# A hybrid decoder step on one core: twelve prepended rows left out of all products after the inputs of convolution and pooling

## The chip, the cores and the metric

The kernel runs on one core of one Trainium2 chip. The metric is the device time of one execution, in microseconds (us). Three runs of the kernel before took 3000.92, 3002.06 and 3005.93 us; their median, 3002.06 us, is the time that the change is measured against.

The engines of the core have the names of the profile: PE multiplies matrices (PEld is its loading of weights, which overlaps), DVE and ACT do the elementwise work, POOL copies a few columns, and SP issues all DMAs, one after the other in its program's order.

## The reference, cut to what matters

One layer over 2064 prompt rows (16 learned rows are prepended to 2048 given ones) and over 64 sample rows (8 sequences of 8 rows, with their past given). D is 1024, F is 2816.

```
xp = concat([meta, x_prompt])                  # 16 + 2048 rows
h = rmsnorm(x, norm1_g);  z = h @ w_in         # 1024 -> 5 * 1024
za, zg, zp, gate_a, gate_b = split(z)
a = causal_dwconv(za * sigmoid(zg), conv_dw)   # 31 taps: row t reads rows t-30 .. t
a = silu(layernorm(a + conv_b)) @ w_conv_out
p = trailing means of zp over 2/4/8/16 rows, minus zp
p = (p @ w_pool, in 4 groups) * pool_scale
x = x + (sigmoid(gate_a) * a + sigmoid(gate_b) * p) @ w_out
up = causal_dwconv(rmsnorm(x, norm2_g) @ w_up, ffn_dw)   # 3 taps: rows t-2 .. t
x = x + (gelu(up[F:]) * up[:F]) @ w_down
y = rmsnorm(x, final_g);  y_prompt = y[16:]    # the 16 prepended rows are dropped
```

Beside y_prompt and y_sample the last rows of the inputs of both convolutions and of the pooling are returned. What a prepended row yields after the convolution and the pooling reaches an output in one way alone: the 3-tap convolution of row 16 reads the up-projected rows 14 and 15. The rows 0 to 13 act through za, zg and zp only.

## The kernel before, in words

Rows of x are the columns of all tiles: a tile is 128 channels by the rows of one block. The 2128 rows (2064 prompt, 64 sample) are cut into three blocks of 708, 708 and 712 (`WIDTHS`); the sample rows end the last one. A product of a block is done in two halves, `hw(b)` columns each, so its matmuls are 354 or 356 columns wide; the up-projection takes two columns more, of the block or half before, for its three taps (`halo=2`): 356 or 358.

Each product is made exact enough by three matmuls of fp32r operands: weights and rows are split into a high and a low part, and `gemm` multiplies low by high, high by low and high by high, for each of the K chunks of 128 and each half:

```
for i, (c0, c1) in enumerate(rng):
    o = ps[:, i, : c1 - c0]
    ...
    mm(o, wl[:, w0 : w0 + P], rh, k == 0, False)
    mm(o, wh[:, w0 : w0 + P], rl, False, False)
    mm(o, wh[:, w0 : w0 + P], rh, False, k == last)
```

`rng(b, ts_, halo)` gives the columns of each half. A unit is one output chunk of 128 channels: for K = 1024 it is 8 x 2 x 3 = 48 matmuls. The units stand in this order: gates and values of block 0, with those of block 1 between (`G_first`); pooling inputs, pooling maps and the two merge gates of block 0 (`PG`), its convolution's output product (`C`), `WO`, and the feed-forward part (`FF`: 44 up units and the down units in four groups); then `PG`, `C`, `WO` of block 1, `G` of block 2, `FF` of block 1; then `PG`, `C`, `WO`, `FF` of block 2. In block 2 all but three of the up-projection's pairs of chunks are done by a Strassen-like scheme of seven half-sized products (`pair`), whose mixed weights are made beforehand on ACT and DVE from `in_w_up` by the task `mixed_weights`: two loads into `raw` tiles, then six parts of it, each with two or more stores `keep<-s`, piece by piece wherever there is room.

Weights are split once, and the halves are stored (`keep<-wb`) and read back later (`wb<-keep`); four buffers `wb` are in use, and SP loads the next as soon as one is free. `final` ends a block: a norm, eight DVE multiplications and eight stores `out_y<-s`.

While it is built, the kernel keeps a model of the engines' time (`Pace`): whenever it holds DVE to be behind PE's planned work, `drip` emits pieces of side tasks (the 31 taps of `conv_norm`, norms, `mixed_weights`). So the place of each such piece in the queues of DVE, ACT and SP hangs on the planned widths. The order within a queue is fixed when the program runs.

In value and pool units `value_post` and `pool_post` write the result behind the history of 30 or 15 columns (zeros for block 0), and pooling's first 16 columns of block 0 are divided by the true count (`icnt`).

Of the kernel before, what the change touches and what calls it, by code (L numbers as in the profile page):

```python
# [26 lines left out]
N_META = 16  # L27
# [4 lines left out]

NBLK = 3
SBLK = 2
TOT = NP_ALL + NSAMP
_W = TOT // NBLK // 4 * 4
WIDTHS = [_W + 4 * (i >= NBLK - (TOT - NBLK * _W) // 4) for i in range(NBLK)]
assert sum(WIDTHS) == TOT and all(w % 4 == 0 for w in WIDTHS)
# [94 lines left out]
def trunk(ctx: ExitStack, tc: tile.TileContext, A, O):  # L133
# [45 lines left out]
    def tt(out, a, b, op):  # L179
        nc.vector.tensor_tensor(out=out, in0=a, in1=b, op=op)  # L180
        pace.put("dve", dve(out, 68 + 60 * (b.space == "PSUM")), [out], [a, b])

    def stt(out, a, s, b, op0, op1):
        nc.vector.scalar_tensor_tensor(out=out, in0=a, scalar=s, in1=b, op0=op0, op1=op1)  # L184
        pace.put("dve", dve(out, 68 if isinstance(s, float) else 129), [out], [a, b])
# [8 lines left out]
    def act(out, a, func, **kw):  # L194
        nc.scalar.activation(out, a, func, **kw)  # L195
        ptr = sum(not isinstance(v, float) for v in kw.values())
        pace.put("act", size(out) / 1.2 + 93 + 93 * ptr + 51 * (a.space == "PSUM"), [out], [a])

    def pcopy(out, a):
        nc.gpsimd.tensor_copy(out, a)  # L200
        pace.put("pool", 220.0, [out], [a])

    def load(out, src):
        nc.sync.dma_start(out=out, in_=src)  # L204
        pace.put("dma", size(out) * P * 4 / 340.0, [out], [], late=2000.0)
# [20 lines left out]
    def hcol(o):  # L226
        return half[:, o - O_LG : o - O_LG + 1]

    def hw(b):
        return WIDTHS[b] // 2  # L230

    def cols(b, ts_):
        return ts_[0] * hw(b), (ts_[-1] + 1) * hw(b)

    def sb(ap, b, ts_):

        c0, c1 = cols(b, ts_)
        return ap[:, c0:c1].rearrange("p (a c) -> p a c", a=len(ts_))

    def ps_of(ps, b, ts_, off=0):  # L240
        return ps[:, : len(ts_), off : off + hw(b)]

    R = {}

# [97 lines left out]
                mm(o, wh[:, w0 : w0 + P], rh, False, k == last)  # L342
            yield

    def rng(b, ts_, halo=0):
        h = hw(b)
        return [(t * h, (t + 1) * h + halo) for t in ts_]


    def at(ap):  # L350
# [74 lines left out]
    def x_load(b, c, c0=0, c1=None):  # L425
        c1 = WIDTHS[b] if c1 is None else c1
        x = S(c1 - c0)
        load(x, A["x"][c, :, COL0[b] + c0 : COL0[b] + c1])
        return x

    def staggered(first):
# [15 lines left out]

    def norm1_first(ts_):

        c0, c1 = cols(0, ts_)  # L450
        xs = [x_load(0, c, c0, c1) for c in range(KC)]
        yield at(xs[0])

        def src(c):
            yield
            return xs[c]

        r = yield from rstd_of(src, c1 - c0)
        if ts_[0] == 0:
            R["h", 0] = [(S(WIDTHS[0], F32R), S(WIDTHS[0], F32R)) for _ in range(KC)]  # L460
# [59 lines left out]

    def gate_post(b, c, ts_, ps):
        if ts_[0] == 0:
            R["t", b, c] = S(WIDTHS[b])
        act(sb(R["t", b, c], b, ts_), ps_of(ps, b, ts_), AF.Tanh, scale=0.5)
        yield

    def value_post(b, c, ts_, ps):
        n, h, t = NPB[b], hw(b), R["t", b, c]
        if ts_[0] == 0:
            a = S(HC + n)  # L530
            pcopy(a[:, :HC], ahist[:, c, :])
            R["a", b, c] = [a, None, 0]
        a = R["a", b, c][0]
        if n == WIDTHS[b]:
            stt(sb(a[:, HC:], b, ts_), sb(t, b, ts_), 1.0, ps_of(ps, b, ts_), ALU.add, ALU.mult)
        else:
# [12 lines left out]
        yield  # L549
# [120 lines left out]
    def pool_post(b, c, ps):  # L670
        W, h, n = WIDTHS[b], hw(b), NPB[b]
        samp = n != W
        g = c // 2
        u = S(HP + n)
        pcopy(u[:, :HP], phist[:, c, :])
        if samp:
            us = R.pop(("su", c))
            act(u[:, HP : HP + h], ps[:, 0, :h], AF.Copy)
            act(u[:, HP + h : HP + n], ps[:, 1, : n - h], AF.Copy)
            act(us[:, :, HP:], ps[:, 1, n - h : h].rearrange("p (a c) -> p a c", a=NS), AF.Copy)  # L680
            store(O["pool_s"][c], us)
        else:
            act(sb(u[:, HP:], b, BOTH), ps_of(ps, b, BOTH), AF.Copy)
        pcopy(phist[:, c, :], u[:, n : n + HP])
        yield at(u)

        def window(u):
# [12 lines left out]
        pf = S(W)  # L700
        inv = 1.0 / WINS[g]
        stt(pf[:, :n], cur[:, HP : HP + n], inv, u[:, HP : HP + n], ALU.mult, ALU.subtract)
        if samp:
            cs = window(us)
            o = pf[:, n:].rearrange("p (a c) -> p a c", a=NS)
            stt(o, cs[:, :, HP:], inv, us[:, :, HP:], ALU.mult, ALU.subtract)
        if b == 0:
            e = mpool.tile([P, 16], F32, tag="e", name=nm("e"), bufs=2)
            tt(e, cur[:, HP : HP + 16], cst[:, O_IC + 16 * g : O_IC + 16 * g + 16], ALU.mult)
            tt(pf[:, :16], e, u[:, HP : HP + 16], ALU.subtract)  # L710
# [408 lines left out]
    def W(key, src, n=None):  # L1119
        wq.append(Weight(key, src, n or src.shape[1]))  # L1120
        return len(wq) - 1
# [8 lines left out]
        t.start, t.after = start, after  # L1130
        order.append(t)

    def std_unit(w, pairs, b, ts_, post, needs=(), wait=False, halo=0, pre=None, drop=None, hold=None):
        box = []

        def mmf(w):
            if pre:
                pre()
            ps = hold.pop() if hold else PSUM()
            (box if hold is None or ts_ == SECOND else hold).append(ps)  # L1140
            yield from gemm(ps if hold is None else ps[:, ts_[0] :, :], w, pairs(), rng(b, ts_, halo))
            if drop:
                del R[drop]

        def after():
            ps = box.pop()
            yield at(ps)
            yield from post(ps)

        units.append(Unit(w, mmf, None if hold is not None and ts_ == FIRST else after, needs, wait))  # L1150

    def gate(b, c, w, nd, ts_=BOTH):
        std_unit(w, lambda: R["h", b], b, ts_, lambda ps: gate_post(b, c, ts_, ps), nd)

    def value(b, c, w, nd, ts_=BOTH, drop=False):
        std_unit(
            w, lambda: R["h", b], b, ts_, lambda ps: value_post(b, c, ts_, ps), nd,
            pre=past(b, "sa", c, HC, "st_conv", 3), drop=("h", b) if drop else None,
        )

    def w_gate(c):
# [437 lines left out]
```

## Time and profile before

| what | us |
|---|---|
| median of three runs | 3002.06 |
| the profiled execution, its own time | 3004.2 |
| its span, first to last instruction | 3002.1 |
| PE busy with matmuls (98% of the span) | 2938.3 |
| PEld busy with weights (97%) | 2924.6 |
| DVE busy (68%) | 2042.8 |
| ACT busy (27%) | 821.2 |
| POOL busy (4%) | 108.8 |

The profiled execution took 2.1 us more than its span and 2.1 us more than the median. The blocks' stages stand at these times: gates and values to 282 us, the rest of block 0 to 1154 us, block 1 (with the gates and values of block 2 within it) to 2150 us, block 2 to the end. Busy shares are means over all of it. A row of the timeline merges instructions of one kind that follow each other closely; "idle before" in brackets is the wait ahead of the first, and what ended it.

### The profile page before, as it was taken

Reading aid. Unit: us, or ns where it says so; the run is one execution under the profiler, and the core shown is the slowest. Engines: PE = TensorE matmul, PEld = TensorE weight load, DVE = VectorE, ACT = ScalarE, POOL = GpSimd, SP = SyncE. Lnnn points to the kernel's source line nnn. Section 1 sums busy time; section 2 is a strip of 40 time slices with the busy share of each in tenths; the row PEclk is TensorE's granted clock in tenths of the full one; section 3 lists DMA queues with packets and bytes.
Section 4 is the critical chain, followed back from the end, with each engine's and each line's share of the span. In section 5 each row is a group of like instructions: output and inputs, shape, how many; then the busy total and the mean of one; then the engine's idle time right before and its main releaser. Section 6 shows DMA issues by size and latency. Waiting matters only on the chain.

```text
span 3002.1 us, 44205 instructions
## 1 busy us (share of the span) xinstructions
PE 2938.3 (98%) x17928; PEld 2924.6 (97%) x17928; DVE 2042.8 (68%) x3006; ACT 821.2 (27%) x1238; POOL 108.8 (4%) x201
## 2 busy tenths in 40 slices
PE   7999999999999998999999999999999999999998
PEld 7999999999999998999999999999999999999997
DVE  7998998679996456653489999655652137544645
ACT  4201334233223232432221212223241113221312
POOL 0111100020000000000010000000000000000000
PEclk9999999999999999999999999999999999999999
DMA  7424554955655557888743444799743376777686
GB/s 283 160 71 161 196 207 162 335 212 173 229 189 197 204 191 286 274 321 277 277 154 120 163 136 146 266 320 328 266 170 138 139 267 215 255 268 263 236 302 242
DMA packets 187755, 660.41 MB, mean 220 GB/s; under 512 B 30880, under 2 KB 39200, under 8 KB 145696
## 3 DMA queue, kind: packets, MB, share of 16 engines
q1 hardware_dynamic: 187552, 657.59, 62.2%
q8 instruction: 141, 2.31, 0.3%
q14 instruction: 62, 0.51, 0.0%
HBM read 433.35 MB, written 224.17 MB: 219 GB/s over the span
## 4 chain that ended last, share of the span: by engine, by line
PE 81%; DVE 12%; ACT 2%; DMA 2%; issue 2%; SPq 0%; DVEq 0%; ACTq 0%
PE ps L212 81%; DVE s L184 8%; DVE s L180 2%; DVE wb L180 2%; ACT s L195 2%; DMA wb<-keep 1%; DMA s<-in_x 0%; ACT wb L195 0%; DMA out_ffn_s<-sf 0%; DMA raw<-in_w_in 0%; SPq L204 0%; DVE s L189 0%; DMA raw<-in_w_dn 0%; SPq L208 0%; DVE rs L184 0%
## 5 line engine op out<-in xcount | busy, mean ns | idle before, releaser
L212 PE MATMUL ps<-s,wb 128*128 128x356 f32 (+2 forms) x17628 | 2904.4, 326 | 32.3 <-DMA wb<-keep 11.7
L212 PEld LDWEIGHTS ps<-s,wb 128*128 128x128 f32 x17628 | 2886.3, 189 | 43.2 <-DVE s L180 19.4
L184 DVE SCALAR_TENSOR_TENSOR s<-s,half,s 128x708 f32<-128x708 f32 (+1 forms) x720 | 622.5, 928 | 0.0
L195 ACT ACTIVATE s<-s 128x708 fp32r<-128x708 f32 (+8 forms) x447 | 316.2, 715 | 829.9 <-DVE s L184 465.8
L180 DVE TENSOR_TENSOR s<-s,s 128x708 f32<-128x708 f32 (+10 forms) x526 | 402.4, 779 | 102.5 <-ACT s L195 92.7
L180 DVE TENSOR_TENSOR s<-s,ps 128x708 f32<-128x708 f32 (+4 forms) x225 | 159.7, 719 | 289.9 <-PE ps L212 233.5
L195 ACT ACTIVATE s<-ps 128x358 f32<-128x358 f32 (+4 forms) x197 | 117.5, 603 | 696.4 <-PE ps L212 679.8
L184 DVE SCALAR_TENSOR_TENSOR s<-ps,cst,s 128x708 f32<-128x708 f32 (+1 forms) x188 | 179.0, 953 | 91.6 <-ACT s L195 88.0
L184 DVE SCALAR_TENSOR_TENSOR s<-s,cst,s 128x712 f32<-128x712 f32 (+3 forms) x188 | 156.5, 845 | 88.2 <-ACT s L195 81.0
L180 DVE TENSOR_TENSOR wb<-raw,wb 128x1024 fp32r<-128x1024 f32 (+3 forms) x136 | 152.9, 1126 | 41.0 <-ACT wb L195 40.6
L195 ACT ACTIVATE wb<-raw 128x1024 fp32r<-128x1024 f32 (+3 forms) x136 | 132.2, 977 | 157.4 <-PE ps L212 92.3
L195 ACT ACTIVATE s<-ps,cst 128x708 f32<-128x708 f32 (+1 forms) x94 | 79.4, 847 | 272.9 <-PE ps L212 266.5
L184 DVE SCALAR_TENSOR_TENSOR s<-s,ps 128x708 f32<-128x708 f32 (+5 forms) x65 | 43.8, 695 | 144.1 <-PE ps L212 124.8
L184 DVE SCALAR_TENSOR_TENSOR s<-s,s 128x708 f32<-128x708 f32 (+2 forms) x96 | 85.5, 891 | 73.4 <-ACT s L195 71.6
L180 DVE TENSOR_TENSOR s<-raw,s 128x512 fp32r<-128x512 f32 x114 | 74.5, 687 | 60.8 <-ACT s L195 52.5
L195 ACT ACTIVATE s<-raw 128x512 fp32r<-128x512 f32 x114 | 68.2, 626 | 86.9 <-DMA raw<-in_w_up 68.7
L180 DVE TENSOR_TENSOR s<-s 128x722 f32<-128x722 f32 (+6 forms) x64 | 55.3, 863 | 28.2 <-ACT s L195 20.5
L200 POOL COPY s<-phist 128x15 f32<-128x15 f32 x24 | 16.5, 687 | 1080.4 <-PE ps L212 1023.8
L184 DVE SCALAR_TENSOR_TENSOR sc<-sa,cst,sc 128x64 f32<-128x64 f32 x232 | 46.9, 280 | 0.3
L195 ACT ACTIVATE s<-s,half 128x708 f32<-128x708 f32 (+1 forms) x48 | 46.5, 975 | 0.8
L195 ACT ACTIVATE s<-s,cst 128x712 f32<-128x712 f32 x38 | 33.7, 886 | 40.4 <-DVE s L180 38.4
L200 POOL CAST s<-hhist 128x2 fp32r<-128x2 f32 x48 | 17.5, 396 | 607.8 <-PE ps L212 389.8
(51 smaller groups left out, 369.5 us busy)
## 6 DMA issues: line engine op xcount, KB each, us to landing
wb<-keep SPq DMA_DIRECT2D x227, 1024.0 KB, 5.0
keep<-wb SPq DMA_DIRECT2D x100, 1024.0 KB, 6.3
keep<-s SPq DMA_DIRECT2D x266, 256.0 KB, 5.7
raw<-in_w_up SPq DMA_DIRECT2D x82, 512.0 KB, 5.7
wb<-keep SPq DMA_DIRECT2D x40, 640.0 KB, 5.2
wb<-keep SPq DMA_DIRECT2D x32, 768.0 KB, 5.2
raw<-in_w_in SPq DMA_DIRECT2D x40, 512.0 KB, 5.2
s<-in_x SPq DMA_DIRECT2D x40, 354.0 KB, 7.6
```

The source lines that it names most:

```text
L180: nc.vector.tensor_tensor(out=out, in0=a, in1=b, op=op)
L184: nc.vector.scalar_tensor_tensor(out=out, in0=a, scalar=s, in1=b, op0=op0, op1=op1)
L195: nc.scalar.activation(out, a, func, **kw)
L200: nc.gpsimd.tensor_copy(out, a)
L212: nc.tensor.matmul(out, lhsT=lhsT, rhs=rhs, start=start, stop=stop, skip_group_check=again)
```

## The change

The first 12 of the 16 prepended rows are taken out of the blocks. The remaining 2116 rows are cut into blocks of 704, 704 and 708. Block 0 has the 12 rows in front as a lead (`SKIP`, `lead(b)`): the first norm of block 0 and its gate, value and pooling-input products run over 716 columns, two halves of 358 (`hx(b)`), and their results for the 12 rows are written into the last 12 columns of the history. The merge gates of block 0 take `h` from column 12 on (`rows="h"`); everything after has 704 columns. Twelve is a multiple of 4 and leaves the rows 14 and 15 that the outputs need.

```diff
-TOT = NP_ALL + NSAMP
+SKIP = 12
+TOT = NP_ALL + NSAMP - SKIP
...
+    def hx(b):
+        return (WIDTHS[b] + lead(b)) // 2
...
-    def rng(b, ts_, halo=0):
-        h = hw(b)
-        return [(t * h, (t + 1) * h + halo) for t in ts_]
+    def rng(b, ts_, halo=0, rows="own"):
+        h = hx(b) if rows == "all" else hw(b)
+        o = lead(b) if rows == "h" else 0
+        return [(o + t * h, o + (t + 1) * h + halo) for t in ts_]
...
-        load(x, A["x"][c, :, COL0[b] + c0 : COL0[b] + c1])
+        load(x, A["x"][c, :, SKIP + COL0[b] + c0 : SKIP + COL0[b] + c1])
...
-            pcopy(a[:, :HC], ahist[:, c, :])
+            pcopy(a[:, : HC - lead(b)], ahist[:, c, : HC - lead(b)])
...
-            stt(sb(a[:, HC:], b, ts_), sb(t, b, ts_), 1.0, ps_of(ps, b, ts_), ALU.add, ALU.mult)
+            stt(sx(a[:, HC - lead(b) :], b, ts_), sx(t, b, ts_), 1.0, px_of(ps, b, ts_), ALU.add, ALU.mult)
...
-            act(sb(u[:, HP:], b, BOTH), ps_of(ps, b, BOTH), AF.Copy)
+            act(sx(u[:, HP - lead(b) :], b, BOTH), px_of(ps, b, BOTH), AF.Copy)
...
-            W(("in", part * KC + c), A["w_in"][part * KC + c]), lambda: R["h", b], b, BOTH, lambda ps: post(b, c, ps), nd, pre=pre, drop=drop
+            W(("in", part * KC + c), A["w_in"][part * KC + c]), lambda: R["h", b], b, BOTH, lambda ps: post(b, c, ps), nd, pre=pre, drop=drop,
+            rows="all" if part == 2 else "h",
```

Gate and value units get `rows="all"`. The program keeps its 17628 matmuls of fp32r operands in the same order, and no instruction is added on DVE or ACT; the widths differ, and pieces of side tasks stand elsewhere.

PE, in `G_first`, where the gate unit of block 0 (chunk 4) is followed by that of block 1 with the same weights `wb_100_631`; before:

```order
L212 MATMUL ps_142_907<-s_51_197,wb_100_631 128x354
L212 MATMUL ps_142_907<-s_50_196,wb_100_631 128x354
L212 MATMUL ps_144_971<-s_114_737,wb_100_631 128x354
L212 MATMUL ps_144_971<-s_115_738,wb_100_631 128x354
L212 MATMUL ps_144_971<-s_114_737,wb_100_631 128x354 x2
```

The same rows now:

```order
L213 MATMUL ps_142_907<-s_51_197,wb_100_631 128x358
L213 MATMUL ps_142_907<-s_50_196,wb_100_631 128x358
L213 MATMUL ps_144_971<-s_114_737,wb_100_631 128x352
L213 MATMUL ps_144_971<-s_115_738,wb_100_631 128x352
L213 MATMUL ps_144_971<-s_114_737,wb_100_631 128x352 x2
```

No matmul moved; block 0's rows of this product became four columns wider, block 1's two narrower.

SP, where block 1 ends and the pooling of block 2 begins: the last two stores of the mixed weights, the eight stores of `final(1)`, and the weights for the units behind the first three of `PG(2)` (`su`, `out_pool_s`: sample rows of the pooling); before:

```order
L208 DMA keep_19190<-s_19191 128x512
L208 DMA keep_19190<-s_19192 128x512
L208 DMA out_y<-s_12543 128x708
L208 DMA out_y<-s_12545 128x708
L208 DMA out_y<-s_12547 128x708
L208 DMA out_y<-s_12549 128x708
L208 DMA out_y<-s_12551 128x708
L208 DMA out_y<-s_12553 128x708
L208 DMA out_y<-s_12555 128x708
L208 DMA out_y<-s_12557 128x708
L204 DMA wb_19305<-keep_2565 128x2048
L204 DMA wb_19307<-keep_2642 128x1024
```

And now, from the sixth of the eight stores on:

```order
L209 DMA out_y<-s_12553 128x704
L209 DMA out_y<-s_12555 128x704
L209 DMA out_y<-s_12557 128x704
L209 DMA keep_19225<-s_19226 128x512
L209 DMA keep_19225<-s_19227 128x512
L205 DMA raw_19232<-in_w_up 128x1024
L205 DMA raw_19233<-in_w_up 128x1024
L205 DMA wb_19254<-keep_2565 128x2048
L205 DMA wb_19256<-keep_2642 128x1024
```

Two stores and two loads of the mixed weights, which had been done earlier, now stand between the stores of y and the first weights.

SP, some 50 us ahead of that, at the last group of down units of block 1 (`keep_6609` holds the first of its weights), where the rows of x for the pooling of block 2 are loaded (`s<-in_x`); before:

```order
L204 DMA raw_18647<-in_w_up 128x1024
L204 DMA s_18717<-in_x 128x712
L204 DMA s_18719<-in_x 128x712
L204 DMA s_18721<-in_x 128x712
L204 DMA s_18723<-in_x 128x712
L208 DMA keep_18725<-s_18726 128x512
L208 DMA keep_18725<-s_18727 128x512
L204 DMA s_18754<-in_x 128x712
L204 DMA s_18765<-in_x 128x712
L204 DMA s_18790<-in_x 128x712
L204 DMA s_18797<-in_x 128x712
L204 DMA wb_18831<-keep_6609 128x2x768
```

And now, to the first of those weights:

```order
L209 DMA keep_18565<-s_18578 128x512
L209 DMA keep_18565<-s_18579 128x512
L205 DMA s_18651<-in_x 128x708
L205 DMA s_18653<-in_x 128x708
L205 DMA s_18655<-in_x 128x708
L205 DMA s_18657<-in_x 128x708
L205 DMA s_18663<-in_x 128x708
L205 DMA s_18692<-in_x 128x708
L205 DMA s_18699<-in_x 128x708
L205 DMA s_18724<-in_x 128x708
L205 DMA wb_18763<-keep_6609 128x2x768
```

The two loads of raw weights and the two stores of mixed ones are gone from between; they come later now.

More of the change, by code (lines that the diff above doesn't have):

```diff
@@ L227, in hcol, with lead @@
         return half[:, o - O_LG : o - O_LG + 1]
+    def lead(b):
+        return SKIP if b == 0 else 0
     def hw(b):
         return WIDTHS[b] // 2
+    def hx(b):
+        return (WIDTHS[b] + lead(b)) // 2
     def cols(b, ts_):
@@ L241, in ps_of, with sx, px_of @@
         return ps[:, : len(ts_), off : off + hw(b)]
+    def sx(ap, b, ts_):
+        return ap[:, ts_[0] * hx(b) : (ts_[-1] + 1) * hx(b)].rearrange("p (a c) -> p a c", a=len(ts_))
+    def px_of(ps, b, ts_):
+        return ps[:, : len(ts_), : hx(b)]
     R = {}
@@ L448, in norm1_first @@
     def norm1_first(ts_):
-        c0, c1 = cols(0, ts_)
-        xs = [x_load(0, c, c0, c1) for c in range(KC)]
+        c0, c1 = ts_[0] * hx(0), (ts_[-1] + 1) * hx(0)
+        xs = [x_load(0, c, c0 - SKIP, c1 - SKIP) for c in range(KC)]
         yield at(xs[0])
@@ L459, in norm1_first @@
         if ts_[0] == 0:
-            R["h", 0] = [(S(WIDTHS[0], F32R), S(WIDTHS[0], F32R)) for _ in range(KC)]
+            R["h", 0] = [(S(2 * hx(0), F32R), S(2 * hx(0), F32R)) for _ in range(KC)]
         def first(c):
@@ L522, in gate_post @@
         if ts_[0] == 0:
-            R["t", b, c] = S(WIDTHS[b])
-        act(sb(R["t", b, c], b, ts_), ps_of(ps, b, ts_), AF.Tanh, scale=0.5)
+            R["t", b, c] = S(2 * hx(b))
+        act(sx(R["t", b, c], b, ts_), px_of(ps, b, ts_), AF.Tanh, scale=0.5)
         yield
@@ L674, in pool_post @@
         u = S(HP + n)
-        pcopy(u[:, :HP], phist[:, c, :])
+        pcopy(u[:, : HP - lead(b)], phist[:, c, : HP - lead(b)])
         if samp:
@@ L708, in pool_post @@
             e = mpool.tile([P, 16], F32, tag="e", name=nm("e"), bufs=2)
-            tt(e, cur[:, HP : HP + 16], cst[:, O_IC + 16 * g : O_IC + 16 * g + 16], ALU.mult)
-            tt(pf[:, :16], e, u[:, HP : HP + 16], ALU.subtract)
+            k = 16 - SKIP
+            tt(e[:, :k], cur[:, HP : HP + k], cst[:, O_IC + 16 * g + SKIP : O_IC + 16 * g + 16], ALU.mult)
+            tt(pf[:, :k], e[:, :k], u[:, HP : HP + k], ALU.subtract)
         hi, lo = S(W, F32R), S(W, F32R)
@@ L1131, in add_task, with std_unit @@
         order.append(t)
-    def std_unit(w, pairs, b, ts_, post, needs=(), wait=False, halo=0, pre=None, drop=None, hold=None):
+    def std_unit(w, pairs, b, ts_, post, needs=(), wait=False, halo=0, pre=None, drop=None, hold=None, rows="own"):
         box = []
@@ L1140, in mmf @@
             (box if hold is None or ts_ == SECOND else hold).append(ps)
-            yield from gemm(ps if hold is None else ps[:, ts_[0] :, :], w, pairs(), rng(b, ts_, halo))
+            yield from gemm(ps if hold is None else ps[:, ts_[0] :, :], w, pairs(), rng(b, ts_, halo, rows))
             if drop:
@@ L1152, in gate @@
     def gate(b, c, w, nd, ts_=BOTH):
-        std_unit(w, lambda: R["h", b], b, ts_, lambda ps: gate_post(b, c, ts_, ps), nd)
+        std_unit(w, lambda: R["h", b], b, ts_, lambda ps: gate_post(b, c, ts_, ps), nd, rows="all")
     def value(b, c, w, nd, ts_=BOTH, drop=False):
@@ L1157, in value @@
             w, lambda: R["h", b], b, ts_, lambda ps: value_post(b, c, ts_, ps), nd,
-            pre=past(b, "sa", c, HC, "st_conv", 3), drop=("h", b) if drop else None,
+            pre=past(b, "sa", c, HC, "st_conv", 3), drop=("h", b) if drop else None, rows="all",
         )
@@ L1542 @@
     samp = I["x_sample"].reshape(NSAMP, D)
-    cut = sum(NPB[: SBLK + 1])
+    cut = SKIP + sum(NPB[: SBLK + 1])
     x = np.concatenate([prompt[:cut], samp, prompt[cut:]], axis=0)
@@ L1559 @@
     arrays = {
-        "x": x.T.reshape(KC, P, TOT),
+        "x": x.T.reshape(KC, P, SKIP + TOT),
         "cst": cst,
@@ L1582 @@
     y = o["y"].reshape(D, TOT).T
-    yp = np.concatenate([y[N_META:cut], y[cut + NSAMP :]], axis=0)[None]
+    cut -= SKIP
+    yp = np.concatenate([y[N_META - SKIP : cut], y[cut + NSAMP :]], axis=0)[None]
     ys = y[cut : cut + NSAMP].reshape(NS, TS, D)
```

## The prediction

> **What bounds the kernel now.** I read the page's sums first, then the waits of PE, then the rate of the matmuls stage by stage, then the few places where PE stands still.
>
> ```profile
> span 3002.1 us, 44205 instructions
> PE 2938.3 (98%) x17928; PEld 2924.6 (97%) x17928; DVE 2042.8 (68%) x3006; ACT 821.2 (27%) x1238; POOL 108.8 (4%) x201
> L212 PE MATMUL ps<-s,wb 128*128 128x356 f32 (+2 forms) x17628 | 2904.4, 326 | 32.3 <-DMA wb<-keep 11.7
> PE ps L212 <- DVE s L180: 28.0, 24, 10.2
> PE ps L212 <- DMA wb<-keep: 11.7, 4, 7.5
> ```
>
> PE is busy 98% of the span. The two largest rows of its waits are 28.0 us for additions of DVE (10.2 of it at the start) and 11.7 us in four waits for weights. So the end is set by how long 17628 matmuls take and by a handful of places. The 326 ns is no rate: matmuls overlap. The rate is the busy time of an unbroken stretch, divided by its count plus one, since the last overhangs by about one period. These are stretches of one width: block 1's merge gates and convolution product; up-projection of block 0; that of block 1; pooling and convolution products of block 2; plain up-projection of block 2.
>
> ```profile
> L212 PE MATMUL ps<-s,wb 128*128 128x354 f32 x708 | 115.6, 325 | 0.0
> L212 PE MATMUL ps<-s,wb 128*128 128x356 f32 x508 | 83.4, 326 | 0.0
> L212 PE MATMUL ps<-s,wb 128*128 128x356 f32 x631 | 103.3, 325 | 0.0
> L212 PE MATMUL ps<-s,wb 128*128 128x356 f32 x1295 | 210.5, 324 | 0.0
> L212 PE MATMUL ps<-s,wb 128*128 128x358 f32 x166 | 27.5, 327 | 0.0
> ```
>
> 115.6/709 is 163.0 ns, then 163.9 and 163.5, then 162.4, and 27.5/167 is 164.7. The reader is to see that the width alone does not order them: 356 columns of block 2 cost no more than 354, and the same 356 cost 1.3 more in the up-projections of blocks 0 and 1. The code tells the two apart: in block 2 both halves begin at a multiple of four columns (0 and 356), in the up-projections the second begins at 354. If a matmul pays for each group of four columns that it touches, 354 at 0 or at 354 and 356 at 0 or 356 all touch 89, but 356 at 354 touches 90, as 358 does. The fourth row against the second and third gives 2 x 1.3 = 2.6 ns for a group (half of those matmuls pay it), the first against them 2 x 0.7 = 1.4, the fifth against the fourth 2.3 and against the first 1.7: I take 2.0 ns, between 1.4 and 2.6.
>
> **The change part by part: widths.** Per stage, counts from the units (48 matmuls for K = 1024):
> - Block 0's gates, values and pooling inputs, 3 x 8 x 48 = 1152, 354 to 358: 163.0 to 164.7, +2.0 us.
> - All else of blocks 0 and 1 but the up-projections, 2688 + 3840 = 6528, 354 to 352. Halves begin at 0 and 352, so 88 groups. No row shows 352; the ends are 0 (354 and 356 cost alike, so narrower may too) and a step of 2.6. The groups fit all five rows, so one step of 2.0: -13.1 us (0 to -17.0).
> - Up-projections of blocks 0 and 1, 2 x 2112 = 4224, 356 to 354, the second half now at 352: from 163.7 to 162.8, the middle of the two rows without the extra group: -3.8 us.
> - Block 2 but for its up-projection, 3840, 356 to 354 at 0 and 354: 162.4 to 163.0, +2.3 us. This third of the product work becomes no cheaper.
> - Block 2's up-projection, 288 + 19 x 84 = 1884, 358 to 356 at multiples of four: 164.7 to 162.4, -4.3 us.
>
> Sum of the widths: -16.9 us. The plain count of columns is another rule: 1152 matmuls gain 4, 16476 lose 2, net 28344 columns less. From first to fifth row the slope is 1.7/4 = 0.42 ns a column, thus -11.9 us. But 356 columns come out below 354 in the fourth row and above them in the second and third, which no count of columns gives: I prefer the groups and keep the count as a rival. The Trainium skill, TensorE: Matmul & The Clock Gate, section "Back-to-back issue gap", has the rule for it: N/2.4 + 2.5 ns for a warm matmul, that is 0.42 ns a column, and an estimate by it is -11.8 us. The trace agrees with its slope between the ends, not with its size: by it 354 columns take 150 ns, and the first row has 163.0.
>
> **DVE, ACT and POOL.** Nearly all their instructions lose four columns.
>
> ```profile
> L184 DVE SCALAR_TENSOR_TENSOR s<-s,half,s 128x708 f32<-128x708 f32 x480 | 424.9, 949 | 0.0
> L184 DVE SCALAR_TENSOR_TENSOR s<-s,half,s 128x648 f32<-128x648 f32 x240 | 197.6, 887 | 0.0
> 477.00:896.00 419.00, 413.90 (x2520) 412.22 (x2519) 358.39 (x447) 138.31 (x178) 19.57 (x32) 0.99 0.61 216
> 900.82 0.88 DVE L180 TENSOR_TENSOR s<-s,ps 128x708 f32<-128x708 f32 x1
> 901.05 2.70 PE L212 MATMUL ps<-s,ones 128*128 128x354 f32 x4 [4.28 <-DVE s L180]
> ```
>
> (949 - 887)/60 is 1.03 ns a column, 4.1 ns for four. This lies beside PE's work and is worth nothing by itself: PE covers it. It matters where PE waits for DVE. The largest such place after the start is the column sums of block 1's convolution, where PE stood 4.28 us; these matmuls keep their place in PE's order. Up to there PE becomes 2323 groups of four shorter (1152 more, 3475 fewer), 4.6 us at 2.0. DVE, busy 358 of the 419 us before (third row, third pair), does 447 instructions there, which save at most 447 x 4.1 ns = 1.8 us, and 1.2 if a third are weight splits and halves; the 240 taps of block 0's convolution ahead of them save 1.0. So of the 4.6 us about 2.4 turn into a longer wait: +2.4 us (0 to 4). The start, with norms and first products four columns wider, has some 50 instructions in a row on ACT and DVE: +0.2 us.
>
> **Moved work at the end of block 1.** SP's order there becomes that of the end of block 0, but for one store. Block 0's end, then block 1's, before:
>
> ```profile
> 1168.03 6.76 SPq L208 DMA_DIRECT2D out_y<-s  x8
> 1173.99 0.68 DVE L180 TENSOR_TENSOR s<-raw,s 128x512 fp32r<-128x512 f32 x1
> 1174.88 1.72 SPq L208 DMA_DIRECT2D keep<-s  x2
> 1176.66 1.33 SPq L204 DMA_DIRECT2D raw<-in_w_up  x2
> 1178.04 0.53 SPq L208 DMA_DIRECT2D keep<-wb  x1
> 1178.97 7.24 SPq L204 DMA_DIRECT2D wb<-keep  x4
> 1188.43 1.81 PE L212 MATMUL ps<-s,wb 128*128 128x354 f32 x5 [7.54 <-DMA wb<-keep]
> ...
> 2163.23 6.70 SPq L208 DMA_DIRECT2D out_y<-s  x8
> 2170.02 5.38 SPq L204 DMA_DIRECT2D wb<-keep  x3
> 2176.41 3.82 PE L212 MATMUL ps<-s,wb 128*128 128x356 f32 x22 [0.41 <-DMA wb<-keep]
> ```
>
> After block 0, behind the stores of y, a pair of stores waited for a DVE subtraction behind the last multiplication, two loads of raw weights and a store followed, and the first weights were issued 4.2 us after SP was done with y; PE stood 7.54 us. After block 1 they went out at once, and PE stood 0.41 us. The DMA engines were full in both, and not after:
>
> ```profile
> 1170.00:1180.00 10.00, 10.00 (x63) 10.00 (x62) 4.83 (x7) 0.76 (x1) 0.13 (x1) 1.00 1.00 353
> 1188.50:1194.40 5.90, 5.90 (x20) 5.90 (x21) 4.21 (x6) 1.95 (x4) 1.03 (x2) 0.50 0.99 411
> 2165.00:2175.00 10.00, 10.00 (x63) 10.00 (x63) 4.27 (x6) 0.88 (x3) 0.00 (x0) 1.00 0.98 353
> 2175.00:2185.00 10.00, 9.59 (x60) 9.33 (x59) 7.93 (x14) 2.88 (x8) 1.97 (x4) 1.00 0.65 203
> ```
>
> ```profile
> 900.00:910.00 10.00, 8.95 (x42) 7.97 (x43) 7.94 (x9) 4.15 (x6) 0.00 (x0) 0.83 0.86 324
> ...
> keep<-s SPq DMA_DIRECT2D x266, 256.0 KB, 5.7
> raw<-in_w_up SPq DMA_DIRECT2D x82, 512.0 KB, 5.7
> keep<-wb SPq DMA_DIRECT2D x16, 768.0 KB, 5.1
> ```
>
> (The last three columns of the windows are granted clock, DMA share and GB/s; the last three rows give the DMAs' sizes.) What stood ahead was 2 x 256 + 2 x 512 + 768 = 2304 KB, and 7.54 - 0.41 = 7.1 us; the change puts 2 x 256 + 2 x 512 = 1536 KB there: by bytes 4.7 us more, a wait of 5.1. The ends are 3.1 (the issue time of the two pairs alone, 1.72 + 1.33) and 7.1 (all of block 0's). Behind the wait the second of these rows shows the clock at 0.50: 20 matmuls in 5.9 us, 2.6 us lost. A wait of 5.1 costs 0 to 2.6 of that; I take 2.0, since the shorter one of 4.28 us at the column sums was followed by a lowered clock too (0.83 over 10 us). Together +6.7 us (3.1 to 9.7).
>
> **The load moved away.** Some 50 us earlier the rows of x had to pass two raw loads and two stores of mixed weights:
>
> ```profile
> 2101.30 1.32 SPq L204 DMA_DIRECT2D raw<-in_w_up  x2
> 2102.73 2.33 SPq L204 DMA_DIRECT2D s<-in_x  x4
> 2107.32 1.05 SPq L208 DMA_DIRECT2D keep<-s  x2
> 2108.43 2.77 SPq L204 DMA_DIRECT2D s<-in_x  x4
> 2111.55 7.47 SPq L204 DMA_DIRECT2D wb<-keep  x4
> 2120.53 35.29 PE L212 MATMUL ps<-s,wb 128*128 128x354 f32 x216 [2.05 <-DMA wb<-keep]
> ```
>
> SP stood from 2105.1 to 2107.3 for the data of these stores, and they took 1.05 us. Without them and without 1536 KB ahead, the weights come at least 3 us sooner: the wait of 2.05 goes, -2.1 us (0 to -2.1; PE has nothing more to gain there).
>
> **Sum:** -16.9 + 2.4 + 0.2 + 6.7 - 2.1 = -9.7 us against the profiled execution's 3004.2 (its span is 3002.1): 2994.5. That execution stands 2.1 above the median of the runs, so 2992.4 for the median.
>
> **The rivals.**
> - No new wait. The weights for the pooling arrive in time in spite of the four DMAs, because fewer bytes are under way than after block 0. For it: in the row of 2165 us the order before left only 0.41 of waiting. Against: SP is serial, and its two pairs alone take 3.05 us. It gives 2992.4 - 6.7 = 2985.7.
> - Columns, not groups: -11.9 in place of -16.9, 2997.4. For it the slope of the ends; against it, 356 below 354 and above it in one kernel.
> - A floor: below 356 columns something else sets about 162.5 ns, for instance the weight loads (97% busy). Then 354 to 352 gains nothing: 2992.4 + 13.1 = 3005.5, no change to speak of. For it the equality of 354 and 356; against it the step to 164.7 two columns on, since a floor lying just there would be chance.
> - Slower: the mixed weights that come later also fill the DMA engines during the pooling of block 2. Fourteen stores and a pair of loads, 4.6 MB, fall on 27 us there, 170 GB/s on top of the 203 of the last row above; the full rows show 353 to 411. If that overflows, each late weight stops PE as after block 0, 7.5 + 2.6 = 10.1 us. Two such beyond the forecast wait give 2992.4 + 20.2 = 3012.6, and from two on it is slower than before. Against it: the sum of both rates still fits, and the weights there are issued three units, 24 us, ahead.
>
> **How the numbers follow.** Groups with the new wait 0.54 (own range 2988 to 2996), no new wait 0.20, columns 0.14, floor 0.08, late weights 0.04. The range 2982 to 3000 holds the first three but for small ends and leaves out the last two, some 0.2. A measurement of this kernel tells 0.2%, 6 us, from no change: faster is below 2996.1. To that go 0.52 of the first, all of the second and 0.05 of the third, 0.77; same 0.18 (most of columns, most of the floor); slower 0.05.
>
> **What would show it.** In the changed kernel's stretches of 352 columns the rate should be 161 ns (163 would be the floor, 162.2 columns); block 0's gates 164.7; block 2's 354 columns 163.0, no faster than its 356 were. PE's waits for weights should lose the one near 2118 us and gain one of 5 us, followed by a half clock, behind the y stores of block 1; the wait at the column sums should be near 6 us. It would be wrong above all if 352 were no cheaper, or if other weights came late.

## The result and the profile after

| | median us | lowest to highest | ratio to before, 95% interval |
|---|---|---|---|
| before | 3002.01 | 3000.92 to 3005.93 | |
| the changed kernel | 2986.49 | 2984.32 to 2988.23 | 0.9946 (0.9928 to 0.9963) |

The change is worth 15.5 us, 0.5%. Its profiled execution took 2984.32 us, 2.2 below its median, where the profiled one of before stood 2.1 above its own: profile against profile the difference is 19.9 us (19.7 in their spans), and the steps below add up to that. The median of before is now that of four runs.

The page of the changed kernel and PE's waits (in us, times, longest):

```profile
span 2982.4 us, 44213 instructions
PE 2914.1 (98%) x17928; PEld 2901.2 (97%) x17928; DVE 2034.0 (68%) x3006; ACT 817.5 (27%) x1238; POOL 106.3 (4%) x201
L213 PE MATMUL ps<-s,wb 128*128 128x354 f32 (+3 forms) x17628 | 2880.9, 325 | 36.3 <-DMA wb<-keep 14.8
PE ps L213 <- DVE s L181: 29.0, 23, 10.0
PE ps L213 <- DMA wb<-keep: 14.8, 5, 7.2
```

PE's matmuls lost 23.5 us (2904.4 to 2880.9), and PE waits 3.1 us more for weights and 1.0 more for DVE. So all of the gain is in the matmuls, and the waits gave a little back.

Stretches of one width, each divided by its count plus one as in the prediction: 352 columns in block 1's convolution product; 354 in the up-projections of block 0 and in pooling and convolution products of block 2; 356 in block 2's up-projection; 358 in block 0's gates:

```profile
L213 PE MATMUL ps<-s,wb 128*128 128x352 f32 x718 | 115.6, 323 | 0.0
L213 PE MATMUL ps<-s,wb 128*128 128x354 f32 x518 | 84.4, 325 | 0.0
L213 PE MATMUL ps<-s,wb 128*128 128x354 f32 x1358 | 220.5, 324 | 0.0
L213 PE MATMUL ps<-s,wb 128*128 128x356 f32 x168 | 27.5, 325 | 0.0
L213 PE MATMUL ps<-s,wb 128*128 128x358 f32 x124 | 20.5, 326 | 0.0
```

That is 160.8, 162.6, 162.3, 162.7 and 164.0 ns. A stretch is one sample of a stage. Over whole stages, the time from one matmul's start to the next one's in both traces, matmul by matmul (stalls and slowed matmuls left out, by keeping 140 to 200 ns), gives for each term of the prediction:

| matmuls | before, ns | after, ns | us | forecast |
|---|---|---|---|---|
| block 0's gates, values, pooling inputs, 1152: 354 to 358 | 163.07 | 164.13 | +1.2 | +2.0 |
| all else of blocks 0 and 1 but up, 6528: 354 to 352 | 162.87 | 160.67 | -14.4 | -13.1 |
| up of blocks 0 and 1, 4224: 356 to 354 | 163.67 | 162.46 | -5.1 | -3.8 |
| block 2 but up, 3840: 356 to 354 | 162.60 | 162.10 | -1.9 | +2.3 |
| block 2's up, 1884: 358 to 356 | 164.66 | 162.09 | -4.8 | -4.3 |
| sum | | | -25.0 | -16.9 |

The end of block 1, in the trace's order of time: SP's stores and loads, PE's wait; below them two windows, the wait and what follows it (the last three columns are granted clock, DMA share, GB/s):

```profile
2144.33 6.45 SPq L209 DMA_DIRECT2D out_y<-s  x8
2150.87 1.09 SPq L209 DMA_DIRECT2D keep<-s  x2
2152.01 1.52 SPq L205 DMA_DIRECT2D raw<-in_w_up  x2
2153.63 2.90 SPq L205 DMA_DIRECT2D wb<-keep  x3
2161.68 8.56 PE L213 MATMUL ps<-s,wb 128*128 128x354 f32 x37 [4.54 <-DMA wb<-keep]
2156.00:2161.00 5.00, 1.14 (x8) 0.85 (x6) 3.89 (x7) 1.52 (x6) 1.00 (x2) 0.90 1.02 408
2161.50:2167.50 6.00, 5.82 (x22) 5.85 (x23) 4.91 (x9) 2.08 (x5) 1.59 (x3) 0.56 0.43 161
```

The two pairs stand between the stores of y and the weights and take 2.6 us of SP; the weights go out 2.8 us after the last store of y, and PE waits 4.5 us while the DMA engines are full. Then the clock is at 0.56: 22 matmuls in 6.0 us, 2.4 us lost against 162.3 ns each.

Some 50 us earlier the rows of x now go out in one piece, and the weights behind them come in time: PE runs on without a wait from 2084.7 to 2112.2 us.

```profile
2084.72 27.49 PE L213 MATMUL ps<-s,wb 128*128 128x354 f32 x171
2084.99 6.64 SPq L205 DMA_DIRECT2D s<-in_x  x8
2092.15 16.44 SPq L205 DMA_DIRECT2D wb<-keep  x5
```

### The profile page after: what moved, and what is told of

The parts are those of the page before. It is cut to its first block, busy times and chain, and to the rows that moved or that the text cites. A ratio compares the mean times of both kernels' runs of the same rounds, so it can differ in the third digit from the quotient of the medians.

```text
span 2982.4 us, 44213 instructions
## 1 busy us (share of the span) xinstructions
PE 2914.1 (98%) x17928; PEld 2901.2 (97%) x17928; DVE 2034.0 (68%) x3006; ACT 817.5 (27%) x1238; POOL 106.3 (4%) x201
## 4 chain that ended last, share of the span: by engine, by line
PE 80%; DVE 14%; DMA 2%; ACT 2%; issue 2%; SPq 0%; DVEq 0%; ACTq 0%
PE ps L213 80%; DVE s L185 9%; DVE s L181 2%; DVE wb L181 2%; ACT s L196 2%; DMA wb<-keep 1%; DMA raw<-in_w_up 0%; SPq L205 0%; DMA out_ffn_s<-sf 0%; ACT wb L196 0%; DMA s<-in_x 0%; DMA raw<-in_w_in 0%; DVE s L190 0%; ACT uhist L196 0%; DVE rs L185 0%
## 5 line engine op out<-in xcount | busy, mean ns | idle before, releaser
L213 PE MATMUL ps<-s,wb 128*128 128x354 f32 (+3 forms) x17628 | 2880.9, 325 | 36.3 <-DMA wb<-keep 14.8
L185 DVE SCALAR_TENSOR_TENSOR s<-s,half,s 128x704 f32<-128x704 f32 (+1 forms) x720 | 619.6, 925 | 0.0
L196 ACT ACTIVATE s<-s 128x704 fp32r<-128x704 f32 (+10 forms) x447 | 314.9, 712 | 817.4 <-DVE s L185 465.8
L181 DVE TENSOR_TENSOR s<-s,s 128x704 f32<-128x704 f32 (+11 forms) x526 | 400.7, 775 | 99.4 <-ACT s L196 88.1
L181 DVE TENSOR_TENSOR s<-s,ps 128x704 f32<-128x704 f32 (+4 forms) x225 | 158.8, 715 | 287.4 <-PE ps L213 229.6
L196 ACT ACTIVATE s<-ps 128x356 f32<-128x356 f32 (+5 forms) x197 | 117.0, 600 | 683.9 <-PE ps L213 662.3
L185 DVE SCALAR_TENSOR_TENSOR s<-ps,cst,s 128x704 f32<-128x704 f32 (+1 forms) x188 | 178.3, 950 | 115.1 <-ACT s L196 111.4
L185 DVE SCALAR_TENSOR_TENSOR s<-s,cst,s 128x708 f32<-128x708 f32 (+4 forms) x188 | 155.9, 842 | 85.0 <-ACT s L196 78.2
L196 ACT ACTIVATE s<-ps,cst 128x704 f32<-128x704 f32 (+1 forms) x94 | 79.1, 844 | 328.1 <-PE ps L213 323.7
L185 DVE SCALAR_TENSOR_TENSOR s<-s,s 128x704 f32<-128x704 f32 (+2 forms) x96 | 85.0, 886 | 69.7 <-ACT s L196 67.8
L181 DVE TENSOR_TENSOR s<-raw,s 128x512 fp32r<-128x512 f32 x114 | 73.8, 686 | 36.7 <-ACT s L196 30.6
```

The lines of the kernel that those rows point to most:

```text
L213: nc.tensor.matmul(out, lhsT=lhsT, rhs=rhs, start=start, stop=stop, skip_group_check=again)
```

## The experiments

All are edits of the changed kernel unless it is said otherwise. "Mean" is the mean from one matmul's start to the next over all of its matmuls of fp32r operands, as in the table; before it is 163.21 ns, in the changed kernel 161.78. One hundredth of a nanosecond is 0.18 us of the whole.

**The order put back.** The planner is told the old widths, so that every queue has the order of before, while the matmuls have the new widths:

```diff
     def size(ap):
...
+        if n in (716, 358):
+            return 708 if n == 716 else 354
+        if n not in (640, 768) and (280 < n < 360 or 600 < n < 760):
+            return n + (2 if n < 400 else 4)
```

> The changed kernel's widths, with every engine's instructions in the order of the kernel before (the planner is told the old widths; no instruction's own width changes). Theory 'order costs': the wait of 4.7 us for weights behind the y stores of block 1 and the half clock behind it (2.6 us) go, the wait of 2.1 us behind the rows of x comes back: 2986.5 - 7.3 + 2.1 = 2981.3 us. Rival 'order is neutral' (what the wait costs is made up elsewhere): 2986.5 us, with a wait of like size at another place.

Measured: 2984.27 us (2982.27 to 2986.61), ratio 0.9943 (0.9928 to 0.9958); mean 161.86 ns. The wait behind the stores of y shrinks from 4.54 to 0.64 us, and the clock stays at 1.00 (third and fourth row); the wait behind the rows of x is back (first two rows, a load of weights on SP, then PE):

```profile
2096.91 7.21 SPq L209 DMA_DIRECT2D wb<-keep  x4
2105.29 4.88 PE L217 MATMUL ps<-s,wb 128*128 128x352 f32 x29 [1.72 <-DMA wb<-keep]
...
2161.09 14.16 PE L217 MATMUL ps<-s,wb 128*128 128x354 f32 x86 [0.64 <-DMA wb<-keep]
2150.00:2170.00 20.00, 19.36 (x120) 19.10 (x119) 12.20 (x20) 4.03 (x11) 2.28 (x6) 1.00 0.79 274
...
PE ps L217 <- DMA wb<-keep: 11.6, 5, 7.4
```

The order moves the waits as forecast, but the two orders differ by 2.2 us in the medians (0.9 by the ratios), and their runs overlap. So the net cost of the moved work, 4.6 us in the prediction, comes out at some 1 to 2; four runs of each exclude neither nought nor, quite, the forecast. This kernel's tiles also lie in other slots than the changed kernel's in nearly half of the matmuls, and its mean is 0.08 ns higher, 1.4 us.

**The distance of the tiles.** The matmuls became 25 us cheaper, 8 more than forecast. Besides the widths one thing had changed that the prediction did not look at: the row tiles (`s`) lie one behind the other in SBUF, and with the longest of them four columns shorter their distance fell from 2976 to 2944 bytes. This kernel puts it back, with the same order, and every tile in the same slot:

```diff
-        t = spool.tile([P, cols], dt, tag="s", name=nm(what))
+        t = spool.tile([P, 738], dt, tag="s", name=nm(what))[:, :cols]
```

> The changed kernel in its own order, but each tile of the big pool takes 738 columns, as before, so that tiles begin 2976 bytes apart (before: 2976; changed kernel: 2944) and every other one starts 32 bytes off a multiple of 64 from its neighbour. Theory 'stride': part of the gain of the matmuls comes from the new spacing, under which all tiles start at one place modulo 64 bytes; rates go back to 162.9 ns at 354, some 161.1 at 352, 162.7 at 356, 164.7 at 358: about +8 us, 2995 us. Rival 'widths alone' (a group of four columns is worth 2.9 ns and the spacing nothing): 2986.5 us, 352 columns at 160.7 ns.

Measured: 2991.44 us (2988.53 to 2993.61), ratio 0.9963 (0.995 to 0.9976), 5.0 us more than the changed kernel, and the two sets of runs don't overlap; mean 162.15 ns. Matmul by matmul, 352 columns cost 0.27 ns more (standard error 0.05), 354 0.28 more, 356 0.78, 358 0.82. So a third of the gain has nothing to do with the work left out. One thing more moves with this edit: the buffers of the weights lie behind the 52 row tiles, so longer tiles push them 52 x 32 = 1664 bytes on. That places in SBUF are worth 0.37 ns is shown; whether it is the tiles' distance or where the rows lie against the weights is not. The terms with the distance of before are +2.2, -12.6, -3.4, -1.4 and -3.4, together -18.6 us.

**The same in the kernel before**: its tiles 3008 bytes apart instead of 2976, so that each begins 32 bytes behind a multiple of 64 (at 2976 every second one does); one tile fewer has room.

```diff
-S_SLOTS = 52
+S_SLOTS = 51
...
-RESERVE = 3
+RESERVE = 2
...
-        t = spool.tile([P, cols], dt, tag="s", name=nm(what))
+        t = spool.tile([P, 752], dt, tag="s", name=nm(what))[:, :cols]
```

> The kernel before with the tiles of the big pool 3008 bytes apart (752 columns, 51 tiles instead of 52, and one fewer held in reserve, so that its order stays word for word): all tiles start at one place modulo 64 bytes, as in the changed kernel; all widths are the old ones. Theory 'stride': 354 columns fall from 162.9 to 162.3 ns, the others by 0.5 to 0.8: 3002.0 - 10 = 2992 us. Rival 'widths alone': 3002 us, 354 columns at 162.9.

Measured: 2999.34 us (2998.18 to 3004.57), ratio 0.9994 (0.9984 to 1.0003); mean 162.93 ns, 0.28 below before. The mean falls by some 4.9 us' worth, half of what likeness against 64 bytes was to bring, and the time can't be told from no change.

**The whole set of tiles moved by 32 bytes**, with the distance of 2944 kept (the constant tile ahead of them is eight columns longer):

```diff
-    half = cpool.tile([P, O_FD - O_LG], F32, tag="half", name="half")
+    half = cpool.tile([P, O_FD - O_LG + 8], F32, tag="half", name="half")[:, : O_FD - O_LG]
```

> The changed kernel with one constant tile eight columns longer, so that the row tiles all begin at a multiple of 64 bytes instead of 32 bytes behind one; spacing 2944 bytes and order unchanged. If only the spacing counts (all tiles alike against 64 bytes): 2986.5, and the rates of 352 and 354 columns stay at 160.7 and 162.3. If the place itself counts: in the run with a spacing of 2976 bytes the 354-column matmuls beginning at a multiple of 64 took 163.0 and those 32 bytes behind it 162.2 ns; then 354 takes 163.0, the mean 162.2 to 162.4 ns, and the time is 2994 to 2997.

Measured: 2986.93 us (2985.91 to 2991.60); mean 161.79 ns, each width within 0.1 of the changed kernel. Moving all the tiles by 32 bytes does not matter. The weights behind them moved along, so the place of the rows against the weights was the same here.

**3008 bytes in the changed kernel**, by the edit that the kernel before got.

> The changed kernel with row tiles of 752 columns, 3008 bytes apart (51 of them instead of 52, order unchanged). They all begin 32 bytes behind a multiple of 64 as in the changed kernel, but fall on four places against 256 bytes instead of two. If alikeness against 64 bytes is what counts: 2986.5, rates 160.7 and 162.3. If the spacing of 2944 bytes is what is cheap: towards the 2991.4 of 2976 bytes.

Measured: 2990.61 us (2988.92 to 2993.07), ratio 0.9958 (0.9943 to 0.9974); mean 162.00 ns. Its mean is 0.22 ns above that of 2944, though all its tiles too lie alike against 64 bytes, and 354 columns took 162.6 ns where that rule gave 162.3. With one slot fewer nearly every tile lies in another slot, so it needed a control:

**51 tiles at 2944 bytes.**

```diff
-S_SLOTS = 52
+S_SLOTS = 51
...
-RESERVE = 3
+RESERVE = 2
```

> The changed kernel with 51 instead of 52 row tiles, 2944 bytes apart as in the changed kernel; the order is the same, but nearly every tile's buffer lies at another of the places than before. It is the control of the run with 3008 bytes, which had these same 51 places. If only the spacing counts: 2986.5, mean of a matmul 161.78 ns. If the place of each tile counts as much: the mean comes out near the 162.0 of the 3008-byte run and the time near 2990.6, and the 4.1 us of that run say nothing on its spacing.

Measured: 2986.17 us (2985.56 to 2987.36), ratio 0.9947 (0.9932 to 0.9961); mean 161.89 ns. The other slots cost 0.1 ns in the mean (0.56 for the 356-column matmuls alone) and no time that can be told. The 3008 run stands 4.4 us above this control (3.3 by the ratios, whose intervals overlap). Of that 0.11 ns, 1.9 us, are in the mean, no more than the slots alone did, and the widths don't agree: 354 columns are 0.37 ns dearer (standard error 0.05), 358 are 0.61 cheaper (0.15), 352 and 356 the same within their errors. PE's idle time ahead of these matmuls is the same in both profiles (36.5 and 36.7 us); the rest is matmuls at half the clock, of which the 3008 profile has some 41 us against 34. So a cost of 3008 bytes is not shown. What is shown is the step between 2976 and 2944, with the same order and the same slots; the control, whose weights lie 2944 bytes nearer to the first row tile at an unchanged distance, moved the mean by 0.1 only, which speaks for the distance but is one place of many. Why 2944 is cheap stays open: it is 23 times 128, and the two others are no multiples of 128, but a second multiple of 128 was not run.

**Groups of four or columns.** First the start: the second half of each 352-column product reads its rows from column 350 on instead of 352 (other columns are multiplied), so that it touches 89 groups of four instead of 88 at the same width.

```diff
             for i, (c0, c1) in enumerate(rng):
+                if i and c1 - c0 == 352:
+                    c0, c1 = c0 - 2, c1 - 2
```

> The changed kernel, in which the second half of each 352-column product reads its rows two columns further left (352 columns at 350 in place of 352; the convolution, output, down and gate products of those halves are those of other rows): as many columns, but 89 groups of four touched instead of 88, by 3072 and some more of the 6528 matmuls. Theory 'groups': stretches of 352 columns rise from 160.7 to 161.6 ns on average, +6 us in all. Rival 'columns': 160.7 ns and no change; 'alignment alone' (a start off a multiple of four costs, however many groups) can't be told apart from groups here: the 354-column matmuls at 354 of block 2 tell that, 162.3 as at 0.

Measured: 2995.01 us, one run. The stretch of block 1's convolution product, half of it shifted:

```profile
L213 PE MATMUL ps<-s,wb 128*128 128x352 f32 x713 | 115.5, 324 | 0.0
```

161.8 ns against 160.8. Over all of them the shifted matmuls (3072; all tiles lie in the same slots as in the changed kernel) take 163.52 ns, the others 160.56: 2.96 ns for a start at an odd pair of columns and the one group more that it brings, at an unchanged count of columns. A count of columns alone is refuted; but the step is larger than the 1.6 ns between 352 and 354 in the changed kernel. The rival that the expectation names, the start alone, can be read from the changed kernel: in block 2 its 354-column matmuls touch 89 groups from either start, and take 161.89 ns from column 0 and 162.30 from column 354. So a start at an odd pair without a group more costs some 0.4, a small part of 2.96.

Then the width at an unchanged count of groups. In block 1, two of each three matmuls become 350 columns wide in `PG`, 348 in `C`, 346 in `WO` (parts of the product are missing in the last columns):

```diff
-                mm(o, wh[:, w0 : w0 + P], rl, False, False)
-                mm(o, wh[:, w0 : w0 + P], rh, False, k == last)
+                mm(o[:, :n], wh[:, w0 : w0 + P], rl[:, :n], False, False)
+                mm(o[:, :n], wh[:, w0 : w0 + P], rh[:, :n], False, k == last)
```

> The changed kernel in which two of the three matmuls of each K chunk are narrower in block 1 only: 350 columns in PG, 348 in C, 346 in WO (the last two to six columns of each half lack these parts of the product). The first of each three keeps 352. By groups of four columns (88, 87 and 87 groups, 1.6 ns each): mean of a stretch 160.7 in PG, 159.6 in C and in WO. By columns (0.42 ns each): 160.1, 159.5 and 159.0. If a floor lies at 160.7: 160.7 in all three. The whole is 2 to 3 us shorter at most.

Measured: 2984.49 us, one run. Against the same matmuls of the changed kernel the narrowed ones cost 0.58 ns less at 350 columns (standard error 0.19, 562 matmuls), 1.84 less at 348 (0.17, 512), 2.17 less at 346 (0.29, 256). Two columns without a change of groups are not free, and the step to 348, with one group fewer, is larger. To settle it, the same for all matmuls of 352 but the first of each product, to 350:

```diff
+                n = c1 - c0 - 2 * (c1 - c0 == 352)
+                m = c1 - c0 if k == 0 else n
+                mm(o[:, :m], wl[:, w0 : w0 + P], rh[:, :m], k == 0, False)
+                mm(o[:, :n], wh[:, w0 : w0 + P], rl[:, :n], False, False)
+                mm(o[:, :n], wh[:, w0 : w0 + P], rh[:, :n], False, k == last)
```

> The changed kernel in which every matmul of 352 columns but the first of a product has 350 (the last two columns of each half lack all but one part of the product); 6192 of 6528 become narrower, none touches fewer groups of four columns. By groups: 160.7 ns and 2986.5 us. By columns, 0.42 ns each: 159.8 ns and 6192 x 0.84 = 5.2 us less, 2981.3. The run with three narrower stretches gave -0.58 for two columns (one stretch of 562), which is nearer to columns.

Measured: 2980.40 us (2979.68 to 2982.72), ratio 0.9926 (0.991 to 0.9943). Block 1's convolution product again, both widths in one stretch (the time per matmul is the larger busy time over the sum of both counts plus one):

```profile
L213 PE MATMUL ps<-s,wb 128*128 128x350 f32 x684 | 114.5, 322 | 0.0
L213 PE MATMUL ps<-s,wb 128*128 128x352 f32 x30 | 9.6, 322 | 0.0
```

160.1 ns against 160.8; over all 6159 that can be paired, 160.08 against 160.63, 0.55 less (standard error 0.05). The narrower widths also changed the planner's order of side work a little, so more than half of the matmuls read another slot than in the changed kernel; among the 3305 that read the same one the difference is 0.48 (0.07). So neither rule holds alone: a column costs 0.24 to 0.28 ns where the groups stay, and the step from 352 to 354, with one group more, is 1.6. The time fell by 6.1 us; 0.55 x 6192 = 3.4 of that is in the matmuls that became narrower, and the rest is not accounted for.

**The mixed weights held back.** If stores and loads ahead of the weights make PE wait, then both block ends must gain when they are kept away. They are held from nine units before `PG(1)` and `PG(2)` to four units into them:

```diff
+        hush = any(mark["PG", b] - 9 <= now["i"] < mark["PG", b] + 4 for b in (1, 2))
-        return posts + ws + [t for t in rest if not (quiet and t.name[0] in ("cv", "sc") or norm and t.name[0] == "mw")]
+        return posts + ws + [t for t in rest if not (quiet and t.name[0] in ("cv", "sc") or (norm or hush) and t.name[0] == "mw")]
```

> The changed kernel, but the mixed weights are held back from nine units before PG(1) and PG(2) begin until four units into them, so that the pooling weights follow the y stores at both block ends; the products are the same. Theory (raw loads and mixed stores ahead of the weights make PE wait): the waits of 7.35 us near 1174 and of 4.70 us near 2157 shrink to under 1 us each, and the half clocks behind them (2.6 and 2.4 us lost) go with them: 2986.5 - 6.6 - 4.0 - 5.0 = about 2971, down to 2973 if half of the lost clock stays. Rival 1: the y stores alone fill the DMA engines, each wait keeps about half: 2979. Rival 2: the work held back makes other weights late (or the sums ahead of the pairs), and the time stays at 2986.

Measured: 2977.81 us (2977.11 to 2979.58), ratio to before 0.9916 (0.99 to 0.9932): 8.7 us faster than the changed kernel, the fastest kernel of all here; mean 161.88 ns, so none of it comes from the rate. The ends of block 0 and of block 1, a window with the granted clock behind each, SP's wait for PE at the end of block 0, and last PE's wait there in the changed kernel:

```profile
1160.80 6.66 SPq L209 DMA_DIRECT2D out_y<-s  x8
1167.55 0.84 SPq L209 DMA_DIRECT2D keep<-wb  x1
1171.62 2.75 SPq L205 DMA_DIRECT2D wb<-keep  x4
1177.72 4.74 PE L213 MATMUL ps<-s,wb 128*128 128x352 f32 x15 [4.20 <-DMA wb<-keep]
...
2140.08 6.84 SPq L209 DMA_DIRECT2D out_y<-s  x8
2147.01 5.16 SPq L205 DMA_DIRECT2D wb<-keep  x3
2153.29 12.00 PE L213 MATMUL ps<-s,wb 128*128 128x354 f32 x72 [0.50 <-DMA wb<-keep]
...
1178.00:1183.00 5.00, 5.00 (x19) 5.00 (x19) 4.08 (x5) 1.44 (x2) 1.02 (x2) 0.55 0.87 364
2140.00:2160.00 20.00, 19.50 (x121) 19.24 (x120) 13.11 (x20) 2.46 (x7) 1.89 (x4) 1.00 0.82 286
...
SPq L205 <- PE ps L213: 4.3, 3, 3.1
...
1181.32 18.95 PE L213 MATMUL ps<-s,wb 128*128 128x352 f32 x100 [7.19 <-DMA wb<-keep]
```

At the end of block 1 the wait fell from 4.5 to 0.5 us and the clock stays at 1.00; at the end of block 0 it fell from 7.2 to 4.2, and the clock is still at 0.55 behind it. There SP, done with the stores at 1168.4, stood until 1171.6 for PE (last row but one, its longest wait, 3.1 us): in this program a load of weights waits for PE until the last matmul that reads the buffer it goes to is done, and four such buffers are in use. Holding back the mixed weights can't remove that, and what is left of the wait and of its lowered clock (4.2 us, and some 2 behind it) is about what the gain falls short of the expected 15. By its time alone the run would fit the first rival (2979), but the waits do not: that one expected about half of each to stay, and one is nearly gone.

## Why the prediction was right, and where a step failed

The forecast was 2992.4 us with a range of 2982 to 3000; the time is 2986.49, inside, and faster by more than 0.2% as held likeliest. It comes out 5.9 us below the forecast. At the tiles' old distance, the only one that the prediction knew, the kernel takes 2991.44, 1.0 from the forecast; some of that closeness is luck, for two terms of the widths miss in opposite directions (below). Point by point:

- **Widths, -16.9.** With the distance of the tiles as before they are worth -18.6 us (second experiment), so the term was nearly of the right size. That sum also holds the price of other slots: 48% of the matmuls read another slot than before, which the run with 51 tiles puts at 0.1 ns, some 2 us either way. 352 columns at 160.7 ns, against the forecast 161, refute the floor (163) and the plain count of columns (162.2). Block 0's gates came out at 164.1 for 164.7.
- **The step inside it that failed: "This third of the product work becomes no cheaper."** Block 2 but for its up-projection became cheaper by 1.9 us (1.4 at the old distance) where +2.3 was forecast; that the other four terms come to -17.2 at the old distance, 2.0 less than their -19.2, made up for half of it. Groups alone were the wrong rule: where the count of groups stays, two columns still take 0.55 ns away. The prediction read the rate of block 2's 356 columns from one stretch (162.4) and that of 354 from block 1 (163.0); the same width differs by 0.5 ns and more between stages and slots.
- **What the sum lacked: the place of the tiles, -5.0 us** in the medians, -6.4 in the means of the profiles (-25.0 against -18.6). The step is that from 2976 to 2944 bytes; the edit that undoes it moves the weights too. The prediction counted what each matmul reads, not where it lies, and no term stood for it. This is nearly all of what the forecast was short by.
- **The new wait, +6.7.** It is there: 4.54 us against 5.1, and 2.4 us lost to the clock behind it against 2.0. (The time lies next to the rival without a new wait, 2985.7, by accident: that rival is the forecast without a wait which is there.) That its causes are the two pairs ahead of the weights is shown by both experiments that take them away: the order put back, where 0.64 us is left, and the mixed weights held back, where 0.5 is left; neither has a lowered clock there.
- **The wait behind the rows of x, -2.1.** It went, and came back with the old order (1.72 us).
- **The column sums, +2.4.** Mis-sized: PE stood 4.80 us there against 4.28. The rows of the changed kernel; then, from the chain of work that leads up to the sums, the last piece of PE in it, before and after:

```profile
895.18 0.88 DVE L181 TENSOR_TENSOR s<-s,ps 128x704 f32<-128x704 f32 x1
895.41 2.10 PE L213 MATMUL ps<-s,ones 128*128 128x352 f32 x3 [4.80 <-DVE s L181]
893.00:903.00 10.00, 7.59 (x29) 6.62 (x30) 8.18 (x10) 4.20 (x5) 0.00 (x0) 0.66 0.98 356
...
636.33 13.22 PE ps L212 x65
...
632.99 12.36 PE ps L213 x65
```

PE got there 6.2 us sooner (896.77 to 890.61), more than the 4.6 of the forecast, but DVE's last addition came 5.6 us sooner too (900.82 to 895.18), not the 2.2 that its shorter instructions were to give. The step that failed is the overlap: the prediction took DVE as a chain of its own over all that time. In the traces the chain that leads to the sums runs over PE until 649.55 us before and 645.35 after, and only from there over DVE (with ACT and a load of weights). So 4.2 us of PE's gain reached DVE as well; behind that point DVE became 1.4 us shorter and PE 2.0, which leaves the 0.5. The clock over 10 us around it was 0.66 (third row; before it was 0.83), so part of the 2.4 us is lost there all the same. This point is read from the two traces; no run isolates it.
- **All waits and slowed matmuls together** come to +5.3 us in the profiles (-19.7 of span less -25.0), against a forecast of +7.2. Late weights during the pooling of block 2, the slower rival, did not show: weights account for five waits in all, and from the new wait at 2161 us to 2409 us PE has none.

What the prediction gave as signs held for the rate of 352, for both waits at the end of block 1 and for block 0's gates; it failed for block 2's 354 columns (162.1 for 163.0) and for the column sums (4.80 for near 6).

Its comparison with the Trainium skill, TensorE: Matmul & The Clock Gate, section "Back-to-back issue gap" (N/2.4 + 2.5 ns, 0.42 ns a column), can now be drawn closer. The section gives this formula for a single warm matmul by itself, and says that in a stream with weight loads it counts too much at large widths; here it counts too little, 150 ns at 354 columns against the 162.9 measured in the kernel before. In slope the runs give 0.24 to 0.28 ns a column where the count of groups stays (352 to 350), less than the formula; between 352 and 354 they give 1.6 for two, twice as much. The formula's single slope lies between both.

## What to carry to other kernels

When a width changes, look at what else follows from it: the distance of the buffers in SBUF changed here by 32 bytes, all that lay behind them moved too, and that was worth a third of the gain, with no instruction changed. Look also at what stands on the loading queue ahead of the weights where a block ends: moving side work away from there was worth 8.7 us, in part because a stop of 4.5 us was followed by a lowered clock that cost 2.4 more. Where two engines feed each other, follow the chain back to the point where the one last waited for the other: what is gained ahead of that point reaches both.

## What the runs showed of the hardware that was not expected

- Where the tiles lie that matmuls read counts: mean 161.78 ns at a distance of 2944 bytes, 162.15 at 2976 with the same order and slots; moving all tiles and the weights behind them together by 32 bytes changes nothing (161.79, and each width the same within 0.1 ns). At 3008 bytes it is 162.00, against 161.89 with the same slots at 2944. The rule behind it is not known, nor whether it is the distance or the place against the weights.
- Which slot a tile lies in moves single groups of matmuls by some tenths of a nanosecond (356 columns of block 2: 162.09 in the changed kernel, 162.66 with 51 slots, 162.87 with the mixed weights held back), while the whole moves by 0.1.
- A start at an odd pair of columns (8 bytes off a multiple of 16) that makes a 352-column matmul touch one group of four more costs 2.96 ns, more than two columns more do; where the count of groups stays, at 354 columns, it costs 0.4.
